# Stacked low-rank products and alternating half-array products in a recurrent branch that runs beside large matrix products

## The chip, the cores and the metric

The kernel runs on one core of one Trainium2 chip. The metric is device time in microseconds (us) of one execution, as a median over runs. The engines are named as in the profile: PE is TensorE (matrix products and transposes), DVE is VectorE, ACT is ScalarE, POOL is GpSimd, SP is SyncE, whose queue issues nearly all DMAs.

## The reference

One layer of a hybrid network on 2048 tokens of 1024 features, in fp32. The recurrent branch is cut to what the change touches.

```python
h = h_res * (1 + sc1) + sh1
proj = h @ w_in + b_in
y_a = gmlp_branch(proj[..., :1024])            # gelu, layer norm, spatial product, u * s
y_b = rwkv7_branch(proj[..., 1024:2720])
merged = sigmoid(gate_a) * (y_a @ w_branch_a) + sigmoid(gate_b) * (y_b @ w_branch_b)
h_res = layer_norm(ALPHA * h_res + gt1 * (merged @ w_out + b_out))
ff = square(relu((h_res * (1 + sc2) + sh2) @ w_ff1 + b_ff1)) @ w_ff2 + b_ff2
out = layer_norm(ALPHA * h_res + gt2 * ff)

def rwkv7_branch(z):                            # 8 heads of 64
    z = z + (shift(z) - z) * mu_shift
    r, k, v, xw, xa, xg = split(z)              # 512, 512, 512, 32, 32, 96
    decay = exp(-exp(-softplus(-(w0 + tanh(xw) @ w_decay_up)) - 0.5))
    a = sigmoid(a0 + xa @ w_aaa_up)             # low rank 32
    g = sigmoid(xg) @ w_gate_up                 # low rank 96
    kk = heads(k * k_k); kk = kk / norm(kk); k = k * (1 + (a - 1) * k_a)
    for t in tokens:                            # state per head: 64 x 64
        state = state * decay_t + (state @ -kk_t) (kk_t * a_t)^T + v_t k_t^T
        y_t = state @ r_t
    return (group_norm(y) + (r * k * r_k).sum() * v) * g
```

## The kernel before

The tokens are worked through in 4 blocks of 512 (TB), each in 4 halves of 128 (HB), each in 2 chunks of 64 (C). The 8 heads are 4 pairs (NP): an even head on partitions 0 to 63, an odd one on 64 to 127.

**Large products.** Every matrix product with a large weight is three products of fp32r operands, each operand split into a high and a low part (`mm3`, lines 453 to 455): high x high, high x low, low x high, each with 512 columns. A generator stands for each stage (`proj_rwkv`, `uv`, `gates`, `merge`, `out_proj`, `second_input`, `ff`) and yields after every 6 large products; one such step is one unit. `fetch` loads a weight tile by a DMA on SP into one of 3 buffers, ACT casts its high part (`whi`, line 387), DVE subtracts for the low part (`wlo`, line 388), again in 3 buffers each.

**Background.** The recurrent branch (`rwkv_a`, `rwkv_b`, `rwkv_c` per half) and `merge_load`, which brings the branches' results in for `merge`, are generators too. `weave` runs them between units of the large products: a background step that yields w is followed by w units (times a factor of 1.0 to 1.3 by block) before the next one. `par` lets rwkv_b of a half run beside rwkv_c of the half before and rwkv_a of the next.

- `rwkv_a` makes, for each head pair, the decays and the scaled keys. `first(p)` starts with two low-rank products of fp32 (lines 587, 588: 64 rows of the array, one PSUM tile `ua`), then works on ACT and DVE. `second(p)` makes the scores: four products (line 625) of 64 rows that use the upper (rows 0 to 63) and the lower half of the array for the even and the odd head, a product with `hones` (626), two transposes (628); DVE takes the results out of PSUM under masks (632, 633). After the pairs one product with `ind` sums the squares of the keys (648).
- `rwkv_b` inverts 32x32 triangles on DVE, then joins them by 16 products of 32x32 for the even and 16 for the odd heads, twice (712, 719: zps, tps).
- `rwkv_c` runs the chunk step: 8 products of the whole array (759, into `xy`), then 8 with the inverse (768, into `us`), 8 with BK (774) and 8 with AB (780), each set first for the even heads, then for the odd ones. A product of fp32 is two passes in the trace. Then `yp` (800, 801) per pair, and the half's result goes to DRAM (`ybd`, line 807).

PSUM has a tag "mm" of four banks for the large products and a tag "rw" of four for the small ones.

Only PE's program order is that of the code (`ORDERED`). The order of the other engines and of the DMA queues is a scheduler's. A weight tile N can be loaded and cast when PE is done with tile N - 6 (three raw and three split buffers).

Of the kernel before, what the change touches and what calls it, by code (L numbers as in the profile page):

```python
# [16 lines left out]
P = 128  # L17
# [72 lines left out]
class Body:  # L90
# [122 lines left out]
    def setup(self):  # L213
# [69 lines left out]
        self.lora = const.tile([C, 2, RW], F32, name="lora")  # L283
        nc.sync.dma_start(out=self.lora, in_=A["lora"])
# [226 lines left out]
    def proj_rwkv(self, b):  # L511
        nc, A = self.nc, self.A
        if self.h_of != b:
            self.go(self.load_h(b))
        xwa = self.work.tile([C, TB], F32, name="xwa", tag="t2", bufs=3)
        pp = self.pre[0] if b == 0 else (yield from self.fm(self.hT, m=C))
        self.shift_mix(pp, C, "xwa", 0, 12, xwa)
        nc.scalar.activation(xwa[0:32], xwa[0:32], AF.Tanh)
        xg = self.work.tile([96, TB], F32, name="xg", tag="t2", bufs=3)
        pp = self.pre[1] if b == 0 else (yield from self.fm(self.hT, m=96))  # L520
        self.shift_mix(pp, 96, "xg", 0, 13, xg)
        nc.scalar.activation(xg, xg, AF.Tanh, scale=0.5)
        nc.vector.tensor_scalar(xg, xg, 0.5, 0.5, op0=ALU.mult, op1=ALU.add)
        xd = self.dr.tile([TB // HB, C + 96, HB], F32, name="xd", tag="xd", bufs=2)
        nc.sync.dma_start(out=xd[:, 0:C].rearrange("h p t -> p h t"), in_=xwa.rearrange("p (h t) -> p h t", t=HB))
        nc.sync.dma_start(out=xd[:, C:].rearrange("h p t -> p h t"), in_=xg.rearrange("p (h t) -> p h t", t=HB))
        zd = [self.dr.tile([TB // HB, P, 3, HB], F32, name=f"zd{p}", tag=f"zd{p}", bufs=2) for p in range(NP)]
        self.spill["z", b] = (xd, zd)
# [25 lines left out]
    def rwkv_a(self, b, h, q):  # L554
# [17 lines left out]
        nc.sync.dma_start(out=xg, in_=xd[h, C:])  # L572
# [7 lines left out]

        def first(p):
            fs = slice(p * P, p * P + P)
            if b == h == 0:
                nc.sync.dma_start(out=zq[:, p], in_=zd[p][h])
            zr, zk, zv = (zq[:, p, j] for j in range(3))
            ua = pst([P, 2, HB], "ua")
            nc.tensor.matmul(ua[:, 0], lhsT=self.lora[:, 0, fs], rhs=xwa, start=True, stop=True)
            nc.tensor.matmul(ua[:, 1], lhsT=self.lora[:, 1, fs], rhs=xwa, start=True, stop=True)
            sg = w1("sg")
            nc.scalar.activation(sg, ua[:, 0], AF.Tanh, scale=0.5, bias=self.w0_h[:, p:p + 1])  # L590
            at = w1("at")
            nc.scalar.activation(at, ua[:, 1], AF.Tanh, scale=0.5, bias=self.a0_h[:, p:p + 1])
            nc.vector.tensor_scalar(sg, sg, 1.0, None, op0=ALU.add)
# [22 lines left out]
            nc.scalar.activation(ksq[:, p], zk, AF.Square, scale=self.vec("k_k", p))  # L616
# [3 lines left out]
        def second(p, bk, kp):  # L620
            zr, zk, zv = (zq[:, p, j] for j in range(3))
            s0, s1 = pst([P, 3, P], "s0"), pst([P, 4, P], "s1")
            for i, sc in enumerate((s0, s1)):
                for c in range(NC):
                    nc.tensor.matmul(sc[:, c], lhsT=bk[half[i], c], rhs=G[i][half[i], p, c], start=True, stop=True)  # L625
            nc.tensor.matmul(s0[:, NC], lhsT=self.hones, rhs=kp, start=True, stop=True)
            for c in range(NC):
                nc.tensor.transpose(s1[:, NC + c], bk[:, c], self.ident)
# [19 lines left out]
        nc.tensor.matmul(ssp, lhsT=self.ind, rhs=ksq, start=True, stop=True)  # L648
        ssq = work.tile([2, NP, HB], F32, name="ssq", tag="ssq", bufs=1)
        nc.scalar.copy(out=ssq, in_=ssp)  # L650
# [13 lines left out]
    def rwkv_b(self, q):  # L664
# [52 lines left out]
        for i, (lo, hi) in enumerate(qd):  # L717
            for u in range(U16):
# [6 lines left out]
    def rwkv_c(self, b, h, q):  # L725
# [20 lines left out]
        for c in range(NC):  # L746
# [8 lines left out]
            xy = pst([P, 2, NP, C], "xy")  # L755
# [5 lines left out]
            Xs = rp.tile([P, NP, C], F32, name="Xs", tag="Xs", bufs=1)  # L761
            nc.vector.tensor_copy(out=Xs[E], in_=xy[E, 0])
            nc.scalar.copy(out=Xs[O], in_=xy[O, 1])
            yield Y_C
            for i in range(2):
                r = half[i]
                for p in range(NP):
# [4 lines left out]
            for i in range(2):  # L772
                for p in range(NP):
# [4 lines left out]
            for i in range(2):  # L778
                for p in range(NP):
                    nc.tensor.matmul(xy[half[1 - i], i, p], lhsT=AB[half[i], p, c, cr[i]:cr[i] + C], rhs=Q[half[i], i, p],  # L780
                                     start=False, stop=True, skip_group_check=True)
            nc.vector.tensor_mul(self.Sc[self.scur], St, PC[:, c][:, :, None].to_broadcast([P, NP, C]))
            nc.scalar.copy(out=Yt[half[c], :, 0], in_=xy[O, 0])
            nc.vector.tensor_copy(out=Yt[half[c], :, 1], in_=xy[E, 1])
# [12 lines left out]
        yb = rp.tile([P, NP, HB], F32, name="yb", tag="yb")  # L797
        for p in range(NP):
            yp = pst([P, 2, HB], "yp")
            nc.tensor.transpose(yp[:, 0], Yt[:, p], self.ident)  # L800
            nc.tensor.matmul(yp[:, 1], lhsT=self.gup[:, p * P:p * P + P], rhs=xg, start=True, stop=True)
# [286 lines left out]
def arrange(np, inp):  # L1088
# [37 lines left out]
    lora = np.zeros((64, 2, 512), w.dtype)  # L1126
    lora[:32, 0] = inp["w_decay_up"][0]
    lora[32:, 1] = inp["w_aaa_up"][0]
    a["lora"] = lora
# [44 lines left out]
```

## Time and profile before

| | |
|---|---|
| time, median of 3 runs | 3103.5 us (3100.29 to 3109.51) |
| time of the profiled execution | 3111.15 us |
| its span, first to last instruction | 3109.3 us |
| mean granted clock of TensorE | 0.993 |
| PE busy (matmul) | 3046.7 us, 98% |
| PEld busy (weight load) | 2455.4 us, 79% |
| DVE busy | 2124.0 us, 68% |
| ACT busy | 1263.4 us, 41% |
| POOL busy | 149.2 us, 5% |

Matmuls overlap in the array, so a row's duration is longer than the distance to the next row's start; the distances tell the pace. An "x16" groups sixteen neighbouring instructions of one line into one row, from the first one's start to the last one's modelled end. The tile of the array that a matmul uses stands as rows*columns behind the names.

### The profile page before, as it was taken

To read this page: it belongs to the slowest core of one execution; us is meant where nothing else is said; L and a number is where in the kernel's file an instruction comes from. 1 tells how busy PE (TensorE), PEld (TensorE's weight loads), DVE (VectorE), ACT (ScalarE), POOL (GpSimd) and SP (SyncE) were. 2 spreads that over 40 slices of the span, in tenths; PEclk is the share of its full clock that TensorE was granted. 3 is DMA by queue.
4 is the path that set the end of the run, shared out by engine and by line. 5 is a ranking of instruction groups with operands and counts; after the bars stand their busy time and mean duration, and the time that the engine had idled before them with its cause. 6 is when DMAs were issued, how large, how long until landed. Compare 5 with 4: busy or idle time off the path is not lost.

```text
span 3109.3 us, 44483 instructions
## 1 busy us (share of the span) xinstructions
PE 3046.7 (98%) x16432; PEld 2455.4 (79%) x16432; DVE 2124.0 (68%) x4727; ACT 1263.4 (41%) x2012; POOL 149.2 (5%) x370
## 2 busy tenths in 40 slices
PE   8999999999999999999999999999999999999998
PEld 6776878777777877878787888787878888888887
DVE  7877874778777686486777657567668755854446
ACT  5534433353343334444433343453444334253332
POOL 1101100000000000100000000110000000000000
PEclk9999999999999999999999999999999999999999
DMA  8565544832323265433323246534333224622332
GB/s 286 158 177 165 169 135 161 271 102 86 98 82 102 82 204 190 152 129 120 104 92 93 89 142 205 164 121 148 118 97 93 84 95 146 223 88 95 98 99 95
DMA packets 241483, 416.71 MB, mean 134 GB/s; under 512 B 72465, under 2 KB 127377, under 8 KB 241265
## 3 DMA queue, kind: packets, MB, share of 16 engines
q1 hardware_dynamic: 241184, 413.59, 41.7%
q8 instruction: 130, 2.13, 0.3%
q14 instruction: 89, 0.72, 0.1%
q0 software_dynamic: 80, 0.26, 0.0%
HBM read 357.60 MB, written 56.17 MB: 133 GB/s over the span
## 4 chain that ended last, share of the span: by engine, by line
PE 85%; DVE 9%; DMA 4%; issue 1%; ACT 1%; SPq 0%; POOL 0%; DVEq 0%; ACTq 0%
PE fm_ps L453 15%; PE fm_ps L455 14%; PE fm_ps L454 14%; PE ff L453 7%; PE ff L454 7%; PE ff L455 7%; PE xy L759 2%; DVE wlo L388 1%; PE ops L454 1%; PE ops L455 1%; PE ops L453 1%; DVE tmp L687 1%; PE s L625 1%; PE vps L453 1%; PE us L768 1%
## 5 line engine op out<-in xcount | busy, mean ns | idle before, releaser
L387 ACT CAST whi<-wraw 128x1024 fp32r<-128x1024 f32 (+1 forms) x500 | 495.0, 991 | 880.7 <-PE fm_ps L454 439.5
L388 DVE TENSOR_TENSOR wlo<-wraw,whi 128x1024 fp32r<-128x1024 f32 (+1 forms) x500 | 573.0, 1148 | 343.2 <-ACT whi L387 335.7
L453 PE MATMUL fm_ps<-xh,whi 128*128 128x512 f32 x1984 | 796.1, 401 | 3.6 <-ACT xh L387 2.2
L454 PE MATMUL fm_ps<-xl,whi 128*128 128x512 f32 x1984 | 774.4, 390 | 2.8 <-DVE xl L388 2.8
L455 PE MATMUL fm_ps<-xh,wlo 128*128 128x512 f32 x1984 | 775.7, 391 | 0.6 <-DVE wlo L388 0.6
L453 PEld LDWEIGHTS fm_ps<-xh,whi 128*128 128x128 f32 x1984 | 370.8, 187 | 91.9 <-issue 5.2
L455 PEld LDWEIGHTS fm_ps<-xh,wlo 128*128 128x128 f32 x1984 | 370.8, 187 | 84.0 <-DVE wlo L388 1.5
L454 PEld LDWEIGHTS fm_ps<-xl,whi 128*128 128x128 f32 x1984 | 371.4, 187 | 77.4 <-DVE xl L388 4.3
L453 PE MATMUL ff<-hh,whi 128*128 128x512 f32 (+1 forms) x1056 | 416.2, 394 | 1.9 <-DVE zr L1051 1.2
L454 PE MATMUL ff<-hl,whi 128*128 128x512 f32 (+1 forms) x1056 | 404.8, 383 | 0.3 <-DVE hl L388 0.3
L455 PE MATMUL ff<-hh,wlo 128*128 128x512 f32 (+1 forms) x1056 | 405.1, 384 | 0.0
L1051 DVE SCALAR_TENSOR_TENSOR zr<-ff,mod,zr 128x512 f32<-128x512 f32 (+1 forms) x264 | 184.9, 730 | 138.6 <-PE ff L455 138.1
L453 PEld LDWEIGHTS ff<-hh,whi 128*128 128x128 f32 x1056 | 198.6, 188 | 46.2 <-issue 6.0
L455 PEld LDWEIGHTS ff<-hh,wlo 128*128 128x128 f32 x1056 | 198.4, 188 | 40.3
L454 PEld LDWEIGHTS ff<-hl,whi 128*128 128x128 f32 x1056 | 198.8, 188 | 35.6 <-DVE hl L388 0.5
L687 DVE TENSOR_TENSOR tmp<-T,L 128x4 f32<-128x4 f32 (+23 forms) x496 | 162.3, 327 | 10.2
L688 DVE TENSOR_REDUCE T<-tmp 128x1 f32<-128x4 f32 (+23 forms) x496 | 122.9, 248 | 10.5
L388 DVE TENSOR_TENSOR hl<-r,hh 128x512 fp32r<-128x512 f32 x128 | 87.7, 688 | 47.8 <-ACT hh L387 47.3
L454 PE MATMUL ops<-wlo,mh 128*128 128x512 f32 x256 | 103.0, 402 | 5.4 <-DVE wlo L388 5.4
L453 PE MATMUL ops<-whi,mh 128*128 128x512 f32 x256 | 102.8, 402 | 1.7 <-DVE ga L914 1.7
L453 PE MATMUL fm_ps<-yh,whi 128*128 128x512 f32 x256 | 102.2, 399 | 1.7 <-ACT yh L387 1.2
L455 PE MATMUL fm_ps<-yh,wlo 128*128 128x512 f32 x256 | 101.5, 397 | 2.0 <-DVE wlo L388 2.0
(236 smaller groups left out, 4018.9 us busy)
## 6 DMA issues: line engine op xcount, KB each, us to landing
wraw<-in_w_ff_dram SPq DMA_DIRECT2D x260, 512.0 KB
wraw<-in_w_gate_dram SPq DMA_DIRECT2D x64, 512.0 KB
wada<-in_w_ada_dram SPq DMA_DIRECT2D x48, 512.0 KB
wraw<-in_w_rkv_dram SPq DMA_DIRECT2D x42, 512.0 KB
gd<-g SPq DMA_DIRECT2D x64, 256.0 KB
ga<-gd SPq DMA_DIRECT2D x64, 256.0 KB
wraw<-in_w_out_dram SPq DMA_DIRECT2D x32, 512.0 KB
zd<-zmix SPq DMA_DIRECT2D x48, 256.0 KB
```

The costliest lines, as they stand in the source:

```text
L387: nc.scalar.copy(out=hi, in_=src)
L388: nc.vector.tensor_sub(lo, src, hi.bitcast(F32))
L453: nc.tensor.matmul(ps, lhsT=wh, rhs=xh, start=start, stop=False)
L454: nc.tensor.matmul(ps, lhsT=wh, rhs=xl, start=False, stop=False)
L455: nc.tensor.matmul(ps, lhsT=wl, rhs=xh, start=False, stop=stop)
L625: nc.tensor.matmul(sc[:, c], lhsT=bk[half[i], c], rhs=G[i][half[i], p, c], start=True, stop=True)
L687: nc.vector.tensor_mul(tmp[:, :n, :w], T[:, :n, :w], L[:, :w, t][:, None, :].to_broadcast([P, n, w]))
L688: nc.vector.tensor_reduce(T[:, :n, t:t + 1], tmp[:, :n, :w], axis=AX.X, op=ALU.add)
L759: nc.tensor.matmul(xy[:, i, p], lhsT=G[i][:, p, c], rhs=Q[:, i, p], start=(i == 0 and p == 0), stop=False, skip_group_check=True)
L768: nc.tensor.matmul(us[r, 0, p], lhsT=TT[r, p * NC + c], rhs=Xs[r, p], start=True, stop=True)
L1051: self.nc.vector.scalar_tensor_tensor(res[:, n, ts], pfs[i], self.mod[:, 40 + n:41 + n], res[:, n, ts], op0=ALU.mult, op1=ALU.add)
```

## The change

- **Low-rank products.** `proj_rwkv` splits xwa into a high and a low part (fp32r) and writes both to DRAM. The weights `lora` are stacked in four groups of 32 rows, twice the high and twice the low part, and `rwkv_a` loads xwa in four pieces to match, so that one product over 128 rows holds the high and low cross terms. For all four pairs the 8 products stand in one run at the half's start, in two PSUM tiles; ACT and DVE turn them into `sgs` and `ats`.
- **Scores.** `second` serves two pairs: 16 passes that alternate between the pair's even and odd head, then the `hones` products, the transposes, and the sums of squares (`ind`), which move here from their own run. `third` takes the results out of PSUM, pair by pair. A run holds four PSUM tiles of tag "rw". The yields change.
- **Inversion.** The two loops of zps and of tps are swapped: even and odd heads alternate.
- **Chunk step.** The 8 products of the whole array become 8 that make only the half that Xs needs (into `us[:, 1]`) and 8 that make the other half (into `xy`), alternating column halves. The loops of the other three sets are swapped so that heads alternate. One copy of 128 partitions makes Xs.
- **Output products.** The four transposes and the four gate products stand in one run with two PSUM tiles.

```diff
-        self.lora = const.tile([C, 2, RW], F32, name="lora")
-        nc.sync.dma_start(out=self.lora, in_=A["lora"])
+        self.lora = const.tile([P, 2, RW], F32R, name="lora")
+        lr = self.sp.tile([P, 2, RW], F32, name="lraw", tag="lraw")
+        for i in range(4):
+            nc.sync.dma_start(out=lr[i * 32:i * 32 + 32], in_=A["lora"])
+        nc.scalar.copy(out=self.lora, in_=lr)
+        nc.vector.tensor_sub(lr[C:], lr[C:], self.lora[C:].bitcast(F32))
+        nc.scalar.copy(out=self.lora[C:], in_=lr[C:])
...
+        parts = [self.work.tile([C, TB], F32R, name=f"xwa{n}", tag="t2", bufs=3) for n in range(2)]
+        self.split(xwa, *parts)
+        for n in range(2):
+            nc.sync.dma_start(out=xs[:, n].rearrange("h p t -> p h t"), in_=parts[n].bitcast(F32).rearrange("p (h t) -> p h t", t=HB))
...
-        xwa = rp.tile([C, HB], F32, name="xwa", tag="xwa", bufs=2)
-        nc.sync.dma_start(out=xwa, in_=xd[h, 0:C])
+        xwa = rp.tile([P, 2, HB], F32R, name="xwa", tag="xwa", bufs=1)
+        for i in range(4):
+            nc.sync.dma_start(out=xwa[i * 32:i * 32 + 32].bitcast(F32),
+                              in_=xs[h, i % 2].rearrange("(a p) t -> p a t", a=2))
...
+        uas = [pst([P, 2, 2, HB], "ua") for _ in range(NP // 2)]
+        for p in range(NP):
+            for i in range(2):
+                nc.tensor.matmul(uas[p // 2][:, p % 2, i], lhsT=self.lora[:, i, p * P:p * P + P], rhs=xwa[:, i],
+                                 start=True, stop=True)
...
-            nc.tensor.matmul(ua[:, 0], lhsT=self.lora[:, 0, fs], rhs=xwa, start=True, stop=True)
-            nc.tensor.matmul(ua[:, 1], lhsT=self.lora[:, 1, fs], rhs=xwa, start=True, stop=True)
...
+        def second(ps_, made):
+
+            sc = {p: (pst([P, 4, P], "s0"), pst([P, 4, P], "s1")) for p in ps_}
+            for p in ps_:
+                for c in range(NC):
+                    for i in range(2):
+                        nc.tensor.matmul(sc[p][i][:, c], lhsT=made[p][0][half[i], c], rhs=G[i][half[i], p, c],
+                                         start=True, stop=True)
+            for p in ps_:
+                bk, kp = made[p]
+                s0, s1 = sc[p]
+                nc.tensor.matmul(s0[:, NC], lhsT=self.hones, rhs=kp, start=True, stop=True)
+                for c in range(NC):
+                    nc.tensor.transpose(s1[:, NC + c], bk[:, c], self.ident)
+
+            for p in ps_:
+                nc.tensor.matmul(sc[p][0][0:2, NC + 1], lhsT=self.ind, rhs=ksqs[p][:, p % 2], start=True, stop=True)
+            return sc
...
-        pend = None
-        for p in range(NP + 1):
-            nxt = first(p) if p < NP else None
-            yield Y_A1
-            if pend:
-                second(p - 1, *pend)
-            pend = nxt
-            yield Y_Z2 if b == h == 0 and 0 < p < NP - 1 else Y_A2
-
-        ssp = pst([2, NP, HB], "ssp")
-        nc.tensor.matmul(ssp, lhsT=self.ind, rhs=ksq, start=True, stop=True)
...
+        for p0 in range(0, NP, 2):
+            for p in (p0, p0 + 1):
+                made[p] = first(p)
+                yield Y_A1 + (Y_Z2 if b == h == 0 and p else Y_A2)
+            sc = second((p0, p0 + 1), made)
+            for p in (p0, p0 + 1):
+                third(p, *sc[p])
+            yield Y_A2
...
-        for i, (lo, hi) in enumerate(qd):
-            for u in range(U16):
+        for u in range(U16):
+            for i, (lo, hi) in enumerate(qd):
...
-                    nc.tensor.matmul(xy[:, i, p], lhsT=G[i][:, p, c], rhs=Q[:, i, p], start=(i == 0 and p == 0),
+
+            for p in range(NP):
+                for i in range(2):
+                    nc.tensor.matmul(us[half[i], 1, p], lhsT=G[i][:, p, c, half[i]], rhs=Q[:, i, p], start=True, stop=True)
+            Xs = rp.tile([P, NP, C], F32, name="Xs", tag="Xs", bufs=1)
+            nc.vector.tensor_copy(out=Xs, in_=us[:, 1])
+            for p in range(NP):
+                for i in range(2):
+                    nc.tensor.matmul(xy[half[1 - i], p], lhsT=G[i][:, p, c, half[1 - i]], rhs=Q[:, i, p], start=p == 0,
                                      stop=False, skip_group_check=True)
...
-            for i in range(2):
-                r = half[i]
-                for p in range(NP):
+            for p in range(NP):
+                for i in range(2):
+                    r = half[i]
                     nc.tensor.matmul(us[r, 0, p], lhsT=TT[r, p * NC + c], rhs=Xs[r, p], start=True, stop=True)
```

Lines of the changed kernel: 459 to 461 are the large products, 596 the low-rank ones, 648 to 658 the score run, 744 and 751 zps and tps, 792 and 797 the split product, 803, 809 and 815 the other three sets of the chunk step.

**PE, a score run of block 0, beside the second block's projection.** Before (`fm_ps` is a large product's PSUM tile, `s` a score tile, `G` the scaled keys of even and odd heads, `bk` and `kp` the other operands):

```order
L455 MATMUL fm_ps<-xh_155,wlo 128x512
L625 MATMUL s_2850<-G_2553,bk 128x128 x2
L625 MATMUL s_2851<-G_2554,bk 128x128 x2
L626 MATMUL s_2850<-kp,hones 128x128
L628 MATMUL s_2851<-ident,bk 128x128 x2
L453 MATMUL fm_ps<-xh_2746,whi 64x512
```

Of the change, from the last two of a run's score products on (eight of two pairs):

```order
L648 MATMUL s_3198<-G_2640,bk 128x128
L648 MATMUL s_3199<-G_2641,bk 128x128
L653 MATMUL s_3196<-kp,hones 128x128
L655 MATMUL s_3197<-ident,bk 128x128 x2
L653 MATMUL s_3198<-kp,hones 128x128
L655 MATMUL s_3199<-ident,bk 128x128 x2
L658 MATMUL s_3196<-ksq,ind 2x128
L658 MATMUL s_3198<-ksq,ind 2x128
L459 MATMUL fm_ps<-xh_2757,whi 128x512
```

One head pair between two large products has become two, with the sums of squares at the end, before the next large product.

**ACT, where the first block's inputs have arrived.** `first` are the PSUM tiles of the opening products, `zraw`, `xwa`, `xg`, `zmix` the mixed inputs made from them, `whi` the high part of a weight tile. Before:

```order
L387 CAST xh_155<-ht 128x512
L387 CAST whi<-wraw 128x1024 x2
L506 ACTIVATE zraw<-first_164,vecs 64x512
L508 ACTIVATE xwa<-first_164,mix 64x512
L506 ACTIVATE zraw<-first_165,vecs 96x512
L508 ACTIVATE xg<-first_165,mix 96x512
L518 ACTIVATE xwa<-xwa 32x512
L506 ACTIVATE zraw<-first_166,vecs 128x512
L522 ACTIVATE xg<-xg 96x512
L508 ACTIVATE zmix<-first_166,mix 128x512
L506 ACTIVATE zraw<-first_167,vecs 128x512
L387 CAST whi<-wraw 128x1024
```

Of the change:

```order
L512 ACTIVATE zraw<-first_164,vecs 64x512
L514 ACTIVATE xwa<-first_164,mix 64x512
L288 CAST lora<-lraw 128x1024
L524 ACTIVATE xwa<-xwa 32x512
L512 ACTIVATE zraw<-first_165,vecs 96x512
L514 ACTIVATE xg<-first_165,mix 96x512
L290 CAST lora<-lraw 64x1024
L528 ACTIVATE xg<-xg 96x512
L393 CAST xwa_558<-xwa 64x512
L512 ACTIVATE zraw<-first_166,vecs 128x512
L512 ACTIVATE zraw<-first_167,vecs 128x512
L393 CAST whi<-wraw 128x1024 x3
```

The casts of the first two weight tiles stood ahead of the first `zraw`; they stand behind it and ten more operations now, among them two casts of `lora` and one of `xwa`.

**SP, the end of block 0.** `wraw<-in_w_a_dram` and `wraw<-in_w_b_dram` are merge's weight fetches in turn, the first of them the 69th tile of the program; `yld` and `uld` are merge_load's loads, `ga` merge's gates, `wada` the modulation weights. Before, from the fourth load of `sd` to merge's fourth weight tile:

```order
L895 DMA yld<-sd 128x512
L375 DMA wada<-in_w_ada_dram 128x1024
L896 DMA uld<-ud 128x512
L899 DMA yld<-ybd 128x512
L912 DMA ga<-gd 128x512
L446 DMA wraw<-in_w_a_dram 128x512
L899 DMA yld<-ybd 128x512
L375 DMA wada<-in_w_ada_dram 128x1024
L880 DMA gd<-g 128x512
L899 DMA yld<-ybd 128x512 x2
L446 DMA wraw<-in_w_b_dram 128x512
```

Of the change, from just ahead of merge's sixth weight tile to its seventh:

```order
L949 DMA ga<-gd 128x512
L950 DMA ga<-gd 128x512
L934 DMA uld<-ud 128x512
L452 DMA wraw<-in_w_b_dram 128x512
L933 DMA yld<-sd 128x512
L934 DMA uld<-ud 128x512
L918 DMA gd<-g 128x512
L937 DMA yld<-ybd 128x512 x3
L381 DMA wada<-in_w_ada_dram 128x1024
L937 DMA yld<-ybd 128x512
L452 DMA wraw<-in_w_a_dram 128x512
```

The last four loads of `ybd` stood before merge's fourth weight fetch; they stand behind its sixth.

## Rows read from the trace of the kernel before

**Rows 1.** The page, part 1: busy time, share of the span, instructions.

```profile
PE 3046.7 (98%) x16432; PEld 2455.4 (79%) x16432; DVE 2124.0 (68%) x4727; ACT 1263.4 (41%) x2012; POOL 149.2 (5%) x370
```

**Rows 2.** Timeline of PE around a run of line 768: start, duration (us), instructions.

```profile
1004.01 0.39 PE L454 MATMUL ff<-hl,whi 128*128 128x512 f32 x1
1004.24 0.39 PE L455 MATMUL ff<-hh,wlo 128*128 128x512 f32 x1
1004.55 0.96 PE L768 MATMUL us<-Xs,TT 64*64 64x64 f32 x16
1005.45 0.50 PE L453 MATMUL ff<-hh,whi 128*128 128x512 f32 x1
1005.78 0.39 PE L454 MATMUL ff<-hl,whi 128*128 128x512 f32 x1
```

**Rows 3.** Timeline of PE in three narrow windows inside that run: passes in flight.

```profile
1004.84 0.44 PE L768 MATMUL us<-Xs,TT 64*64 64x64 f32 x7
...
1005.12 0.39 PE L768 MATMUL us<-Xs,TT 64*64 64x64 f32 x4
...
1005.24 0.28 PE L768 MATMUL us<-Xs,TT 64*64 64x64 f32 x2
```

**Rows 4.** Timeline of PE around lines 774 and 780.

```profile
1008.41 0.97 PE L774 MATMUL us<-Q,BK 128*64 128x64 f32 x16
1009.30 0.96 PE L780 MATMUL xy<-Q,AB 64*64 64x64 f32 x16
```

**Rows 5.** Timeline of PE around line 759.

```profile
999.92 1.89 PE L759 MATMUL xy<-Q,G 128*128 128x64 f32 x16
1001.62 0.48 PE L453 MATMUL ff<-hh,whi 128*128 128x512 f32 x1
```

**Rows 6.** Timeline of PE around an inversion run.

```profile
1543.33 1.09 PE L712 MATMUL zps<-T,AB 32*32 32x32 f32 x32
```

**Rows 7.** Timeline of PE around a low-rank run.

```profile
1508.61 0.48 PE L587 MATMUL ua<-xwa,lora 64*128 64x128 f32 x2
...
1509.25 0.50 PE L453 MATMUL ff<-hh,whi 128*128 128x512 f32 x1
```

**Rows 8.** Timeline of PE around the transposes of v.

```profile
1567.25 0.60 PE L738 MATMUL vt<-ident,zq 128*128 128x128 f32 x4
1567.60 0.48 PE L453 MATMUL ff<-hh,whi 128*128 128x512 f32 x1
```

**Rows 9.** Timeline of PE around a score run.

```profile
1522.59 0.72 PE L625 MATMUL s<-G,bk 64*128 64x128 f32 x8
1523.24 0.49 PE L626 MATMUL s<-kp,hones 128*128 128x128 f32 x2
...
1523.70 0.48 PE L453 MATMUL fm_ps<-xh,whi 128*128 128x512 f32 x1
```

**Rows 10.** Timeline of PE around the sums of squares.

```profile
1564.80 1.02 PE L648 MATMUL ssp<-ksq,ind 128*2 128x512 f32 x2
```

**Rows 11.** Timeline of ACT and of PE where the first block's inputs end.

```profile
56.48 0.69 ACT L506 ACTIVATE zraw<-first,vecs 64x512 f32<-64x512 f32 x1 [4.13 <-PE first L455]
...
61.14 0.39 PE L453 MATMUL fm_ps<-xh,whi 128*128 128x512 f32 x1
```

**Rows 12.** Timeline of PE at the second block's first product; brackets: idle time, releaser.

```profile
283.46 0.69 PE L454 MATMUL fm_ps<-xl,whi 128*64 128x512 f32 x1 [2.21 <-DVE xl L388]
```

**Rows 13.** Windows: length, busy of PE, PEld, DVE, ACT, POOL, then granted clock, DMA.

```profile
282.50:289.20 6.70, 5.74 (x15) 3.15 (x15) 5.99 (x12) 3.79 (x7) 0.00 (x0) 0.50 0.47 152
```

**Rows 14.** Timeline of SP, DVE and PE at the end of block 0.

```profile
543.71 0.32 SPq L896 DMA_DIRECT2D uld<-ud  x1
...
548.36 0.69 DVE L388 TENSOR_TENSOR yl<-yld,yh 128x512 fp32r<-128x512 f32 x1 [0.69 <-ACT yh L387]
...
558.74 0.40 PE L453 MATMUL fm_ps<-yh,whi 128*128 128x512 f32 x1
```

**Rows 15.** Groups of instructions of DVE: busy us, mean ns, idle before, releasers.

```profile
L632 DVE TENSOR_TENSOR AB<-s,mask_e 64x256 f32<-64x256 f32 x64 | 26.4, 413 | 17.4 <-PE s L626 16.7
```

More of the change, by code (lines that the diff above doesn't have):

```diff
@@ L615, in first, with third @@
                 nc.vector.tensor_mul(bk[r, :, cr[i]:cr[i] + C], ch(kp)[r], ch(pinv)[r])
-            nc.scalar.activation(ksq[:, p], zk, AF.Square, scale=self.vec("k_k", p))
+            nc.scalar.activation(ksq[:, p % 2], zk, AF.Square, scale=self.vec("k_k", p))
             nc.vector.scalar_tensor_tensor(kp, kp, self.vec("r_k", p), zr, op0=ALU.mult, op1=ALU.mult)
             return bk, kp
-        def second(p, bk, kp):
-            zr, zk, zv = (zq[:, p, j] for j in range(3))
[L622 to L628, printed above, removed]
+        def second(ps_, made):
[14 more added lines that the diff above has]
+            return sc
+        def third(p, s0, s1):
+            zr, zk, zv = (zq[:, p, j] for j in range(3))
             for i, sc in enumerate((s0, s1)):
@@ L636, in second @@
             nc.scalar.copy(out=BK[:, p], in_=s1[:, NC:])
-        pend = None
-        for p in range(NP + 1):
-            nxt = first(p) if p < NP else None
-            yield Y_A1
-            if pend:
-                second(p - 1, *pend)
-            pend = nxt
-            yield Y_Z2 if b == h == 0 and 0 < p < NP - 1 else Y_A2
-        ssp = pst([2, NP, HB], "ssp")
-        nc.tensor.matmul(ssp, lhsT=self.ind, rhs=ksq, start=True, stop=True)
-        ssq = work.tile([2, NP, HB], F32, name="ssq", tag="ssq", bufs=1)
-        nc.scalar.copy(out=ssq, in_=ssp)
+            nc.scalar.copy(out=ssq[:, p], in_=s0[0:2, NC + 1])
+        ssq = work.tile([2, NP, HB], F32, name="ssq", tag="gsq", bufs=1)
+        made = {}
+        for p0 in range(0, NP, 2):
[6 more added lines that the diff above has]
+            yield Y_A2
         U = NP * NC
@@ L716, in rwkv_b @@
         yield Y_V2
-        for i, (lo, hi) in enumerate(qd):
-            for u in range(U16):
+        for u in range(U16):
+            for i, (lo, hi) in enumerate(qd):
                 nc.tensor.matmul(tps[lo, u], lhsT=Zs[hi, u], rhs=TT[hi, u, 32:64], start=True, stop=True)
@@ L777, in rwkv_c @@
             self.scur ^= 1
-            for i in range(2):
-                for p in range(NP):
-                    nc.tensor.matmul(xy[half[1 - i], i, p], lhsT=AB[half[i], p, c, cr[i]:cr[i] + C], rhs=Q[half[i], i, p],
+            for p in range(NP):
+                for i in range(2):
+                    nc.tensor.matmul(xy[half[1 - i], p], lhsT=AB[half[i], p, c, cr[i]:cr[i] + C], rhs=Q[half[i], i, p],
                                      start=False, stop=True, skip_group_check=True)
             nc.vector.tensor_mul(self.Sc[self.scur], St, PC[:, c][:, :, None].to_broadcast([P, NP, C]))
-            nc.scalar.copy(out=Yt[half[c], :, 0], in_=xy[O, 0])
-            nc.vector.tensor_copy(out=Yt[half[c], :, 1], in_=xy[E, 1])
+            nc.scalar.copy(out=Yt[half[c], :, 0], in_=xy[O])
+            nc.vector.tensor_copy(out=Yt[half[c], :, 1], in_=xy[E])
         yv = Yt.rearrange("p k h i -> p (k h) i")
@@ L797, in rwkv_c @@
         yb = rp.tile([P, NP, HB], F32, name="yb", tag="yb")
+        yps = [pst([P, 2, 2, HB], "yp") for _ in range(NP // 2)]
         for p in range(NP):
-            yp = pst([P, 2, HB], "yp")
-            nc.tensor.transpose(yp[:, 0], Yt[:, p], self.ident)
-            nc.tensor.matmul(yp[:, 1], lhsT=self.gup[:, p * P:p * P + P], rhs=xg, start=True, stop=True)
+            nc.tensor.transpose(yps[p // 2][:, p % 2, 0], Yt[:, p], self.ident)
+        for p in range(NP):
+            nc.tensor.matmul(yps[p // 2][:, p % 2, 1], lhsT=self.gup[:, p * P:p * P + P], rhs=xg, start=True, stop=True)
+        for p in range(NP):
+            yp = yps[p // 2][:, p % 2]
             y1 = rp.tile([P, HB], F32, name="y1", tag="t1", bufs=1)
```

51 lines of the change are left out of this document (24 added, 27 removed).

## The prediction

> **What bounds the kernel now.** The page's busy times come first: PE, TensorE's matmul queue, is busy for 98% of the span [rows 1]. There is almost no idle time to win, so a gain has to come from fewer or cheaper PE instructions, and any new wait of PE costs its full length. The next view is PE's timeline, row by row around one small run. The large products (N=512) follow each other every 0.23 us. A run of small ones between two of them starts 0.31 us after the last large one instead of 0.23, when it uses only part of the array, and the first large product behind it needs 0.33 until its follower starts [rows 2]. I price every run as entry + its own time to the first large product + exit - 2 x 0.23, that is, as what PE would save if the run vanished.
>
> The same view shows how parts of the array work together. In the run of line 768 eight products use the upper left quarter of the array, then eight the lower right one. Asked for narrow windows, the timeline gives 4 passes in flight near the end, where only the second quarter works, and two of them start within 0.12 us, so 0.06 apart; near the middle, where the end of one set meets the start of the other, it gives 7 [rows 3]. Passes have the same length, so both quarters were working at once, at nearly double rate. The queue reaches ahead only a little, so most of each set still runs alone. Alternating the quarters should give the double rate throughout.
>
> **The change, part by part.**
>
> Chunk step (32 of them: 4 blocks, 4 halves, 2 chunks).
> - Line 768 now costs 0.31 + 0.90 + 0.33 - 0.46 = 1.08 us [rows 2]. Alternated: 8 pairs of passes at 0.06 = 0.48, plus 0.09 behind the last (1005.12 to 1005.45 less four passes [rows 2, 3]) and about 0.05 for the first, so 0.31 + 0.62 + 0.33 - 0.46 = 0.80. Saves 0.28 x 32 = 9.0.
> - Lines 774 and 780 stand in one run: 0.89 and, less a tail of 0.06 as in rows 2, 0.90 us [rows 4], 1.98 with entry and exit. Alternated, 0.62 each: 1.42. Saves 0.56 x 32 = 17.9.
> - Line 759 (full array, 64 columns of output per pass) takes 1.70 [rows 5], with entry 0.23 and exit 0.33 1.80. It becomes 32 passes of half the array's columns, in 16 pairs: 0.96 + 0.14, with entry and exit 1.28. Saves 0.52 x 32 = 16.6.
>
> Inversion (zps and tps, 32 runs). 32 passes take 1.09 us less 0.06 of tail [rows 6], 1.21 with entry and exit. At 0.032 per pass, 16 pairs take 0.51 + 0.14, with entry and exit 0.83. Saves 0.38 x 32 = 12.2.
>
> Low-rank products. A run of lines 587 and 588 takes 0.64 us [rows 7], 0.82 with entry and exit, and there are 64: 52.5. Now 8 one-pass products with the whole array make one run per half. No row shows an fp32r pass of 128 columns. The nearest is the transpose, one pass of the same tile: four take 0.35 [rows 8], so eight 0.70, 0.80 with entry and exit, x 16 = 12.8. Saves 39.7. Bounds: at a quarter of a 512-column pass each (0.06) they would save 44; as dear as the old products (0.64 / 2) they would save 10. I take the transpose, since it has the same tile and the same single pass.
>
> Scores. A run for one head pair takes 1.11 us to the next large product [rows 9], 1.29 with entry and exit, 64 times; the sums of squares (ssp) take 0.95 after their tail [rows 10], 1.14 in all, 16 times: together 100.8. The new run serves two pairs: 2 x 1.11, less one change of tile shape (an estimated 0.20: eight passes take 0.65 to line 626, of which 0.45 go at the average pace of rows 4), plus that change and about 0.32 for the four narrow passes of ind, and 0.10 more behind a narrow tile: 2.82 with entry and exit, x 32 = 90.2. Saves 10.6. The score passes already alternate quarters, so alternation gives nothing here.
>
> The output products (yp) keep their passes in fewer runs; with a full-array entry at the normal spacing I count nothing. The 32 Xs copies that ACT loses and the DVE copy that gets 128 partitions are hidden behind the twelve large products between two runs; without that cover they cost about 0.3 each, 10 us. Each half's four loads of xwa instead of one, and each block's extra write and split, go to SP, ACT and DVE before PE asks for them, but for the first half (below).
>
> Work removed: 9.0 + 17.9 + 16.6 + 12.2 + 39.7 + 10.6 = 106 us.
>
> New waits, against it.
> - Start. In ACT's new order eleven operations stand ahead of the first weight cast, which used to run before them. The first starts at 56.48 after waiting for PE, and PE needs the weights at 61.14 [rows 11]. Nine at about 0.65 (0.69 with the overlap) and two double-width casts at an estimated 1.0 end at 64.4, the cast at 65.4, plus the VectorE half: about 5 us late. Behind a pause of 2.21 us at the second block's first product [rows 12] the granted clock stood at 0.50, the lower of its two levels (1.2 and 2.4 GHz), for 6.7 us [rows 13]; that costs 3.35 in full, 1.7 for half the stretch. The low-rank run also waits for its new loads, queued on SP behind weight fetches. I take 8 us in all, between 3 and 12.
> - End of blocks 0 and 1. rwkv_a has 28 units instead of 25, so the last yp of block 0 comes 60 large products later, 48 before merge. SP's order shows what follows: the last loads of y stand behind merge's sixth weight fetch, whose buffers come free when PE is done with the last gates tile, which is when merge starts (558.74). From a load of u to the end of its split took 543.71 to 549.05, 5.3 us [rows 14]; with the queue ahead of it 7, and 2.5 for the clock (between 0 and 3.35). Block 1 has the same shape. Together 19, between 5 and 25. Blocks 2 and 3 have over 200 large products of slack.
> - Middle. A pair run takes all four banks of the tag "rw", and rwkv_b, rwkv_c and the next run ask for the same four. They come free after third: four products at 0.41 [rows 15] and about 0.3 for the last, 2.0 us of DVE per head pair, 4.0 per run. The next asker is mostly 2 to 5 units (1.4 us each) behind, but DVE is also doing splits and inversions. I take 0.3 per run, 10 us, between 0 and 64.
>
> The sum is 8 + 19 + 10 = 37 of waits, -69 net. The profiled execution took 3111.15 (span 3109.3), so 3042 for it; it lies 7.6 above the median of the runs, 3103.5, so I predict 3035.
>
> A rule of the Trainium skill speaks against the alternation. TensorEngine Tiling (Array Packing), Restrictions and Gotchas, Gotcha 1, says that different row tiles cannot access the same PSUM bank simultaneously. Lines 768, 780 and the inversions write one bank from two row tiles. The seven passes in flight speak against it here: there the row tiles wrote one bank, in different partitions. By the row these three save 9.0, 9.0 and 12.2; by the rule it is the rival "row tiles take turns" below.
>
> **The rivals.**
> - Waits stay hidden (0.12). For it: nearly every wait of PE now is short, and background work has slack. Against it: the ACT order at the start. -106: 2998.
> - Banks wait (0.07): each pair run exposes one pair's evacuation, 2.0 x 32 = 64 in place of 10: -106 + 27 + 64 = -15, 3088. For it: all four banks are held. Against it: the askers stand some units behind.
> - Banks wait in full, the other side (0.04): all 4.0 us of third stand in PE's way at each of 32 runs, 128: +49, 3152. It decides from 2.5 us per run on ((106 - 27) / 32).
> - Row tiles take turns (0.02): lines 768 and 780 then cost 16 x 0.06 + 0.14 in place of 0.90, 0.20 more each, the inversions 0.13 more, each x 32, and they save nothing: -106 + 30 + 17 + 37 = -22, 3082. Rows 3 speak against it.
> - No overlap at all (0.02): the runs of 759 and 774 lose theirs as well, so the split of 759 costs 0.44 x 32 = 14 and 774 0.21 x 32 = 7 instead of saving 16.6 and 9: -106 + 30 + 17 + 26 + 21 + 37 = +25, 3128. Rows 3 speak against it, and so does 774: its two sets of eight take 0.89, less than 16 x 0.06 + 0.14.
>
> **How the numbers follow.** The forecast, gain of 106 against waits of 20 to 60 and dearer low-rank passes, has 0.70 and its own range 3013 to 3062. 0.03 is for what I have not seen. The range over all reaches to 2997 (half of the hidden-waits case) and to 3080; left out are the other half, most of the bank cases, and the last rival, about 0.2. A measurement of this kernel can tell about 0.3%, 9 us, from no change. Faster than 3094: the forecast, hidden waits, row tiles and most of one pair's banks, 0.90; within 9 us 0.04; slower 0.06.
>
> **What would show it.** The run of 803 at 0.6 us from its first pass to the next large product, that of 809 with 815 at about 1.3, that of 792 with 797 near 1.1, the eight low-rank products near 0.7: each is right or wrong by itself in PE's timeline. The waits: PE idle for the first weights near 61 us, idle at the first product of merge in blocks 0 and 1, with granted clock 0.50 behind each. If PE's waits name s, zps or xy banks through DVE for tens of us, the bank case holds. The forecast is wrong if 792 and 797 take more than 1.7 us, or if waits sum to over 100.

## The result and the profile after

The changed kernel takes 3072.1 us (median of 4 runs, 3068.8 to 3075.0) against 3104.4 before; the ratio is 0.9895, 95% interval 0.9877 to 0.9913. That is a gain of 32 us, less than half of the 69 forecast. The profiled execution took 3075.0 with a span of 3073.3, 36.0 under the span of before.

The page's busy times, which answer to [rows 1]:

```profile
PE 2963.9 (96%) x16912; PEld 2396.8 (78%) x16912; DVE 2127.0 (69%) x4684; ACT 1247.6 (41%) x2028; POOL 157.0 (5%) x370
```

PE is busy 83 us less, but the span is only 36 shorter: 47 us of idle time are new. The timeline of PE shows the runs themselves, in the second half of the span, where nothing waits (start, duration, instructions):

```profile
1482.41 0.68 PE L803 MATMUL us<-Xs,TT 64*64 64x64 f32 x16
1483.02 0.50 PE L459 MATMUL fm_ps<-xh,whi 128*128 128x512 f32 x1
...
1485.97 0.69 PE L809 MATMUL us<-Q,BK 128*64 128x64 f32 x16
1486.58 0.68 PE L815 MATMUL xy<-Q,AB 64*64 64x64 f32 x16
1487.19 0.50 PE L459 MATMUL fm_ps<-xh,whi 128*128 128x512 f32 x1
...
1510.47 1.00 PE L596 MATMUL ua<-xwa,lora 128*128 128x128 f32 x8
1511.31 0.44 PE L459 MATMUL ff<-hh,whi 128*128 128x512 f32 x1
...
1533.24 1.16 PE L648 MATMUL s<-G,bk 64*128 64x128 f32 x16
1534.33 0.49 PE L653 MATMUL s<-kp,hones 128*128 128x128 f32 x2
1534.66 0.38 PE L655 MATMUL s<-ident,bk 128*128 128x128 f32 x2
1534.87 0.39 PE L653 MATMUL s<-kp,hones 128*128 128x128 f32 x2
1535.10 0.38 PE L655 MATMUL s<-ident,bk 128*128 128x128 f32 x2
1535.41 0.60 PE L658 MATMUL s<-ksq,ind 128*2 128x128 f32 x4
1535.94 0.50 PE L459 MATMUL fm_ps<-xh,whi 128*128 128x512 f32 x1
...
1542.97 0.69 PE L744 MATMUL zps<-T,AB 32*32 32x32 f32 x32
1543.59 0.50 PE L459 MATMUL ff<-hh,whi 128*128 128x512 f32 x1
...
1573.92 0.69 PE L792 MATMUL us<-Q,G 128*64 128x64 f32 x16
1574.43 0.64 PE L797 MATMUL xy<-Q,G 128*64 128x64 f32 x16
1575.00 0.50 PE L459 MATMUL fm_ps<-xh,whi 128*128 128x512 f32 x1
```

From a run's first pass to the next large product: 803 takes 0.61 (forecast 0.62; [rows 2] 0.90), 809 with 815 1.22 (1.24; [rows 4] 1.79), 792 with 797 1.08 (1.10; [rows 5] 1.70), the inversion 0.62 (0.65; [rows 6] 1.03), the eight low-rank products 0.84 (0.70). The score run of two pairs takes 2.70, 2.90 in all where 2.82 was forecast. With these figures the work removed is 9 + 18 + 17 + 12 + 38 + 8 = 102 us, not 106. That side came out nearly as priced; of the 102, 66 us were lost elsewhere, since the span is 36 shorter.

Where, the windows tell. The stretches end where PE starts the first large product of merge in block 0, of second_input in block 0, of merge in block 1, of block 2's projection, of merge in blocks 2 and 3. Before:

```profile
0.00:558.74 558.74, 533.79 (x3064) 420.41 (x3065) 409.54 (x1074) 236.34 (x392) 55.08 (x142) 0.99 0.58 180
558.74:658.03 99.29, 92.34 (x396) 72.85 (x394) 73.71 (x125) 33.56 (x47) 2.42 (x7) 1.00 0.64 212
658.03:1115.87 457.84, 453.76 (x2702) 364.37 (x2703) 352.67 (x906) 192.95 (x350) 15.84 (x41) 0.99 0.32 98
1115.87:1218.60 102.73, 96.95 (x417) 77.21 (x416) 83.96 (x141) 39.14 (x56) 4.10 (x8) 0.97 0.63 210
1218.60:1880.30 661.70, 660.66 (x3643) 532.11 (x3642) 434.25 (x991) 277.10 (x445) 30.66 (x78) 1.00 0.37 116
1880.30:2639.10 758.80, 755.17 (x4058) 608.64 (x4057) 514.17 (x1126) 313.47 (x495) 34.24 (x83) 1.00 0.40 128
```

After (columns as in [rows 13]: length, busy of PE, PEld, DVE, ACT, POOL, then granted clock):

```profile
0.00:557.04 557.04, 515.20 (x3184) 407.52 (x3184) 406.70 (x1061) 233.59 (x396) 52.58 (x142) 0.97 0.57 179
557.04:668.90 111.86, 98.62 (x395) 74.90 (x395) 77.78 (x129) 35.59 (x49) 2.42 (x7) 0.91 0.61 203
668.90:1114.10 445.20, 430.44 (x2823) 348.09 (x2823) 352.84 (x893) 189.37 (x354) 22.05 (x41) 0.98 0.33 97
1114.10:1225.20 111.10, 99.77 (x416) 78.42 (x417) 85.28 (x143) 39.78 (x57) 3.87 (x7) 0.92 0.65 211
1225.20:1865.20 640.00, 635.47 (x3761) 515.71 (x3760) 434.21 (x980) 271.10 (x448) 32.91 (x78) 1.00 0.39 120
1865.20:2603.00 737.80, 730.16 (x4178) 592.15 (x4177) 514.64 (x1115) 307.33 (x498) 36.29 (x83) 1.00 0.43 132
```

Each of stretches 1, 3, 5 and 6 holds one block's recurrent branch and lost 102 / 4 = 25.5 us of work. They are shorter by 1.7, 12.6, 21.7 and 21.0; the two around merge, which lost no work, are longer by 12.6 and 8.4. So the shortfall is 24 in block 0, 13 in merge behind it, 13 in block 1, 8 in its merge, and 4 and 5 in the last two. Of the first 24 and the 13 of block 1, 3.5 and 1.1 are a wait for y just ahead of merge's first product, which the windows count to the stretch before it. Behind merge of block 3 the two kernels run alike. In the short stretches the granted clock is lower too: 0.91 and 0.92 at the two merges, against 1.00 and 0.97.

Three places where PE waits, from its timeline: the first weights, the first low-rank run, and the start of merge in block 0, five times there (idle time and releaser in brackets):

```profile
64.10 0.79 PE L459 MATMUL fm_ps<-xh,whi 128*128 128x512 f32 x1 [3.66 <-ACT whi L393]
...
75.70 0.78 PE L596 MATMUL ua<-xwa,lora 128*128 128x128 f32 x4 [1.84 <-DMA xwa<-xs]
...
557.04 0.58 PE L459 MATMUL fm_ps<-yh,whi 128*128 128x512 f32 x1 [3.49 <-ACT yh L393]
...
563.36 0.79 PE L459 MATMUL fm_ps<-yh,whi 128*128 128x512 f32 x1 [4.36 <-ACT yh L393]
...
567.23 0.80 PE L459 MATMUL fm_ps<-yh,whi 128*128 128x512 f32 x1 [1.92 <-ACT yh L393]
...
571.04 0.79 PE L459 MATMUL fm_ps<-yh,whi 128*128 128x512 f32 x1 [1.86 <-ACT yh L393]
...
574.08 0.79 PE L459 MATMUL fm_ps<-yh,whi 128*128 128x512 f32 x1 [1.09 <-ACT yh L393]
```

The granted clock (column behind POOL) at the first and the third of them, from the windows:

```profile
62.38:69.20 6.82, 4.89 (x11) 3.40 (x12) 5.12 (x6) 5.09 (x8) 1.47 (x4) 0.50 0.60 152
557.31:577.79 20.48, 11.00 (x20) 5.40 (x20) 9.05 (x15) 5.01 (x8) 0.00 (x0) 0.50 0.68 237
```

At merge four tiles of y come one after the other, the second 6 us behind the first, the next two 4 us apart, while PE needs all four for its first twelve products. Through these 20.5 us the clock is at 0.50.

In block 1 PE waits 6.05 us for a PSUM bank of the feed-forward sum, which `zr` on DVE has to take out. DVE's timeline shows what stood ahead of `zr`: the evacuation of a pair run (taking its results out of PSUM, 666 to 669) between steps of the inversion (719, 720), without a pause. The last of it, of DVE, then of PE:

```profile
785.24 0.43 DVE L666 TENSOR_TENSOR AB<-s,mask_o 64x256 f32<-64x256 f32 x1
785.70 0.60 DVE L719 TENSOR_TENSOR tmp<-T,L 128x256 f32<-128x256 f32 x1
786.32 0.42 DVE L667 TENSOR_TENSOR G<-s,mask_o 64x256 f32<-64x256 f32 x1
786.66 0.40 DVE L720 TENSOR_REDUCE T<-tmp 128x8 f32<-128x256 f32 x1
786.99 0.27 DVE L669 TENSOR_TENSOR zq<-s,zq 128x128 f32<-128x128 f32 x1
787.19 1.39 DVE L1089 SCALAR_TENSOR_TENSOR zr<-ff,mod,zr 128x512 f32<-128x512 f32 x2
...
788.07 0.77 PE L459 MATMUL fm_ps<-xh,whi 128*128 128x512 f32 x1 [6.05 <-DVE zr L1089]
```

### The profile page after: what moved, and what is told of

Same layout as the page of the kernel before. It is cut to its first block, busy times and chain, and to the rows that moved or that the text cites. A ratio compares the mean times of both kernels' runs of the same rounds, so it can differ in the third digit from the quotient of the medians.

```text
span 3073.3 us, 45399 instructions
## 1 busy us (share of the span) xinstructions
PE 2963.9 (96%) x16912; PEld 2396.8 (78%) x16912; DVE 2127.0 (69%) x4684; ACT 1247.6 (41%) x2028; POOL 157.0 (5%) x370
## 4 chain that ended last, share of the span: by engine, by line
PE 57%; DVE 3%; DMA 1%; ACT 1%; issue 0%; SPq 0%; DVEq 0%; ACTq 0%
PE fm_ps L459 10%; PE fm_ps L460 10%; PE fm_ps L461 10%; PE ff L459 6%; PE ff L460 6%; PE ff L461 6%; PE ops L460 1%; PE ops L461 1%; PE ops L459 1%; DVE wlo L394 1%; PE s L648 1%; PE vps L459 0%; PE vps L461 0%; PE vps L460 0%; PE pf L460 0%
## 5 line engine op out<-in xcount | busy, mean ns | idle before, releaser
L460 PE MATMUL fm_ps<-yl,whi 128*128 128x512 f32 x256 | 105.2, 411 | 1.4 <-DVE yl L394 1.1
```

The source lines that it names most:

```text
L460: nc.tensor.matmul(ps, lhsT=wh, rhs=xl, start=False, stop=False)
```

## The experiments

Times are medians of runs beside the kernel before on the same chip (3102.3 to 3106.6 by group); a gain is against that.

**The chunk step and the inversion alone.** The kernel before with the changed loops of `rwkv_b` and of the chunk step, as in the diff above, and nothing else.

> The kernel before with the chunk step and the inversion of the change, nothing else. Theory W (the work comes off as priced, and the waits that ate it belong to the pair runs of scores with their later output products): the runs save (1.99 + 1.79 + 1.09 - 1.43 - 1.28 - 0.81) x 32 = 43 and 0.40 x 32 = 13, and nearly no wait is added: 3104 - 56 = 3048, at most 3057. Rival F (a faster PE by itself runs into DVE, ACT and the loads, whatever part makes it faster): half of it is lost, 3062 to 3080.

3056.7, a gain of 47.6 (ratio 0.9841, 0.9824 to 0.9858): most of the 56, as W has it and not F, and 15 us faster than the whole change. By stretch block 0 takes 543.2 and merge behind it 97.0, and block 1 takes 446.7: blocks 0 and 1 gave back 15.5 and 11.2 of the 14 that each lost in work, though DVE is busy for 75% and 79% of them.

**The low-rank products alone.**

```diff
+        uas = [pst([P, 2, 2, HB], "ua") for _ in range(NP // 2)]
...
-        ksq = rp.tile([P, NP, HB], F32, name="ksq", tag="ksq", bufs=1)
+        ksq = ats
```

> The kernel before with the stacked low-rank products alone (splits, loads and setup of the change; scores of one pair per run; squares of the keys go into the tile of the second tanh once it is used). W: saves (0.84 x 64 - 0.90 x 16) = 39, loses about 10 at the start (late weight cast, late load, clock): 3075. Rival F: 3085 to 3095. Rival L (the extra loads and splits of this part carry the waits of the change): 3095 or more, with PE waiting for xwa in many halves.

3093.6, a gain of 10.7 of 39. W missed by 19, and PE waits for xwa only once, 1.7 us, so L does not hold as it was put; the result lies in F's range.

**The change without the pair runs.** `second(p, bk, kp)`, the loop with `pend` and `ssp` as before.

> The change with the scores as before (one pair per run, sums of squares apart, yields of 25 units per half; squares as in the run above). W: 56 + 39 of work saved, 10 to 15 of waits at the start and in between, no train of waits at the first products of merge in blocks 0 and 1: 3020 to 3026. Rivals F and L: the waits stay, 3050 to 3075.

3064.3, a gain of 40.1. The trains at merge (waits for y, one behind the other) are gone (101.7 and 99.6 us for the two merge stretches), as W has it, but two parts that gain 47.6 and 10.7 alone gain 40.1 together. The pair runs, priced at 8 us of gain, cost 8: by stretch 10.1 and 11.5 at the two merges and 1.0 and 4.1 in blocks 0 and 1, while blocks 2 and 3 take 8.0 and 6.4 longer without them. The time lies in F's range and not in W's. But of the 20 us that the two parts together lack in the profiles, 12 are in blocks 2 and 3, where each has one new wait for `zr`, with a granted clock of 0.74 over the next 6.6 us and of 0.62 over the next 6.7:

```profile
1604.46 0.47 PE L459 MATMUL fm_ps<-xh,whi 128*128 128x512 f32 x1 [4.39 <-DVE zr L1075]
...
2347.82 0.77 PE L459 MATMUL fm_ps<-xh,whi 128*128 128x512 f32 x1 [5.39 <-DVE zr L1075]
```

Such a wait needs neither a pair run nor the blocks in which DVE is fullest.

**A tighter background.**

```diff
-LAT0 = 1.05
-LAT1 = 1.0
+LAT0 = 1.0
+LAT1 = 0.95
```

> The change with the background of blocks 0 and 1 set 5% tighter (LAT0 1.05 to 1.0, LAT1 1.0 to 0.95), so that the last output products come 78 and 72 large products earlier, 18 and 36 earlier than in the kernel before. W: the trains of waits at merge in blocks 0 and 1 (13.5 and 9.9 us idle, with the clock halved behind) go, some of it comes back as waits of scores for DVE: 3045 to 3055. Rival: the trains have another cause (loads late for SP's queue, not for the output products), 3068 to 3075.

3047.3, a gain of 57.0, 25 us better than the change. The merge stretches take 98.5 and 100.8, so the trains are gone, and merge of block 0 starts without a wait:

```profile
556.05 0.39 PE L461 MATMUL fm_ps<-xh,wlo 128*128 128x512 f32 x1
556.28 0.40 PE L459 MATMUL fm_ps<-yh,whi 128*128 128x512 f32 x1
```

The trains came of the output products' place: the last of block 0 stand 126 large products ahead of merge here, 48 in the change, 108 in the kernel before.

**The setup of lora early.** The load, casts and subtraction of `lora` stand ahead of `self.first_tiles()`; tried on the change, on the low-rank part alone, on the change with the tighter background, and on the change without pair runs.

```diff
+        nc.scalar.copy(out=self.lora, in_=lr)
+        nc.vector.tensor_sub(lr[C:], lr[C:], self.lora[C:].bitcast(F32))
+        nc.scalar.copy(out=self.lora[C:], in_=lr[C:])
         self.first_tiles()
```

> The change with the load, casts and subtraction of lora written ahead of the opening products, so that ACT's casts of the first two weight tiles stand ahead of the first zraw again. Theory S (the late weight casts at 61 us start a backlog of ACT, loads and clock that runs on through block 0): most of the 25 us that block 0 fell short up to merge come back, 3052 to 3060. Rival D (block 0 falls short since DVE, ACT and SP have as much to do per large product there as PE, whatever the start): only the start's own wait and clock come back, some 6 us, 3064 to 3068.

> The kernel before with the stacked low-rank products alone, their setup ahead of the opening products. Priced: 39 us of work. S: 3070 to 3080, with block 0 no longer behind the kernel before at its merge. D: 3084 to 3090.

> The change with the tighter background of blocks 0 and 1 (LAT0 1.0, LAT1 0.95) and the setup of lora early. If the trains of waits at merge and the start are apart, both gains add: 3047 less 12 to 20 by S, 3028 to 3036; less 6 by D, 3039 to 3043.

> The change with scores of one pair per run as before and the setup of lora early. S: 3064 less 12 to 20, 3044 to 3052, which would be the best without touching the background's pace. D: 3056 to 3060.

3070.2, 3087.8, 3042.1 and 3057.1: 2, 6, 5 and 7 us better than without. The wait of 3.66 for the first weights is gone, but the opening products start 2.1 to 2.6 us later, and the first low-rank run waits longer for xwa (3.83 in place of 1.66 in the low-rank part alone). Theory S, a backlog that runs on from the late weight casts, falls: with them in time little comes back. The edit moved part of the start's loss to xwa and did not remove it.

**DVE relieved.** Every second step of the inversion is left out, in the change and, as a control, in the kernel before; the 32x32 inverses are then not computed in full.

```diff
-        for t in range(1, 32):
+        for t in range(1, 32, 2):
```

> The change with every second step of the triangle inversion left out (two DVE operations each; about 34 us of DVE per block; the inverse is not computed in full, the yields and PE's order stay). Theory D (in blocks 0 and 1 PE waits since DVE's queue is nearly as full as PE's): the waits for bk, for zr and for Yt shrink, block 0 and block 1 each get 5 to 12 us faster: 3072 to 3050 or lower. Rival P (the waits come from loads, ACT and PE's order alone): 3068 to 3074.

> The control: the kernel before with the same steps left out. D: PE there waits little for DVE (some 10 us in the background's stretches), so it gains at most 8 us, clearly less than the change does: 3096 to 3103. If it gains as much as the change, DVE's load is not what the change runs into.

The change comes to 3045.2, 27 us less; the control to 3094.4, 12 less. The difference is in blocks 0 and 1: their stretches shrink by 15.6 and 13.3 us in the change, by 8.1 and 5.4 in the control. In the change PE's waits (total, times, longest) name DVE's `bk` and `zr`:

```profile
PE s L648 <- DVE bk L637: 6.4, 6, 2.4
PE fm_ps L459 <- DVE zr L1089: 6.1, 1, 6.1
```

With DVE relieved that for `bk` is not in the list any more, and that for `zr` is halved:

```profile
PE fm_ps L459 <- DVE zr L1089: 3.2, 1, 3.2
```

The merge stretches stay as long (111.7 and 110.1), so they are another matter. D holds, for about 15 of the 37 us that blocks 0 and 1 fell short (28.9 less the control's 13.5). The control gained more than D had it (12, not 8): DVE held PE up a little before as well.

**Tiles of their own for the loads of y.**

```diff
-            y = work.tile([P, TB], F32, name="yld", tag="t2", bufs=3)
+            y = bp.tile([P, TB], F32, name="yld", tag=f"ml{k}")
...
-                u = work.tile([P, TB], F32, name="uld", tag="t2", bufs=3)
+                u = bp.tile([P, TB], F32, name="uld", tag=f"mh{k}")
```

> The change with tiles of their own for the loads of y and u before merge (in the space of the merge results, which are not yet made) in place of the three that everything shares. Theory T (the waits at merge's start are four loads in a row, each waiting for the tiles of the one before): the trains of 13.5 and 9.9 us become one wait each, 6 to 8 us, with less half clock behind: 3072 less 15 to 25, 3047 to 3057. Rival Q (SP's queue holds the loads back, behind weight fetches): 3066 to 3074.

3058.1, 14 us better than the change; T at block 0, less than it gave in all. At merge of block 0 the train is a wait of 3.35 and small ones, at that of block 1 one of 8.21:

```profile
556.35 0.51 PE L459 MATMUL fm_ps<-yh,whi 128*128 128x512 f32 x1 [3.35 <-ACT yh L393]
...
557.68 0.80 PE L460 MATMUL fm_ps<-yl,whi 128*128 128x512 f32 x1 [0.82 <-DVE yl L394]
...
560.81 0.80 PE L459 MATMUL fm_ps<-yh,whi 128*128 128x512 f32 x1 [0.63 <-ACT yh L393]
...
1112.23 0.79 PE L459 MATMUL fm_ps<-yh,whi 128*128 128x512 f32 x1 [8.21 <-ACT yh L393]
```

The merge stretches take 103.7 and 107.1. The wait of 8.21 counts to the stretch ahead of merge, which grows from 445.2 to 452.2, so block 1 with its merge is 3 us longer than in the change, and block 0 with its merge 9 shorter. The stretches of blocks 2 and 3 shrink too, 640.0 to 635.8 and 737.8 to 730.5, which is their full price: there `ff` had shared its three tiles with the late loads of y, and its two waits of 1.7 for `hh` are gone.

**Together, and kp on ACT.** Early setup, tighter background, own tiles, and

```diff
-            nc.vector.tensor_scalar(kp, at, self.ka_h[:, p:p + 1], self.ka_c[:, p:p + 1], op0=ALU.mult, op1=ALU.add)
+            nc.scalar.activation(kp, at, AF.Identity, scale=self.ka_h[:, p:p + 1], bias=self.ka_c[:, p:p + 1])
```

> The change with the early setup of lora, the tighter background (3042 together), the own tiles for y and u, and the scaling of kp moved from DVE to ACT (64 operations, 21 us of DVE). D and T: 5 to 10 us under 3042 by the lighter DVE, nearly nothing by the tiles since the output products already come in time there: 3032 to 3038. P: 3040 to 3044.

3025.5 (ratio 0.9736, 0.9721 to 0.9750), better than expected: a gain of 81 against 102 of work removed. How much of the 17 us over the version without the last two edits belongs to either was not tried apart; in the profiles blocks 2 and 3 give 4.3 and 6.4 of it, about what the own tiles gave there alone.

**The low-rank part once more, by pair and with DVE relieved; the fastest version started later.** The first keeps two stacked products per head pair at their old places, each pair's in a PSUM tile of its own.

> The kernel before with the stacked low-rank products, setup early, but two products per head pair at the places of before, in a PSUM tile each. By rows a run of two costs about 0.3 (0.23 + 0.2 + 0.32 - 0.46) x 64 = 19 in place of 52, so 33 priced against 39 in one run per half. Theory U (the run of eight takes two banks at once at the half's start, waits for them and for xwa, and is why the low-rank part alone returned 16 of 39): 3070 to 3078. Rival D (the stretch is short of DVE and ACT time whatever the places): 3084 to 3094.

> The low-rank part alone with early setup (3088), with every second step of the triangle inversion left out. The same edit took 10 to 12 off the kernel before and 27 off the change. D: clearly more than 12 off, 3064 to 3072. U: 10 to 12 off, 3075 to 3078.

> The fastest version so far (3026) with the first half's background started three units later (Y_Z 4 to 7), so that the first low-rank run does not wait 5.7 us for xwa. If that wait and the half clock behind it are all, 3017 to 3021; if the later start is only passed on to the waits behind, 3024 to 3028.

3088.1, as with one run per half: U falls, the place and the banks are not the cause. With DVE relieved 3073.3, 14.5 less, hardly more than the control's 12 and in neither theory's range: the low-rank part's own shortfall is not shown to be DVE's. By stretch (early setup) it is in block 0, 562.4 against 558.7 before, where 10 had to come off, and some 3 us in block 1; blocks 2 and 3 gain their 10 each. Set against the kernel before product by product, it falls behind in three steps: 6 us where the first low-rank run waits 3.83 for xwa, 5 where the spatial product waits 3.02 for `u` on ACT and the next product 1.51 for `sv` on DVE, and 5 where the next low-rank run waits 2.28 and, for `yb` on DVE, 1.68. The later start brings block 0's merge forward by 6.5 us in the profile and the time to 3023.3 from 3025.5, too little to tell: stretches 2, 3 and 6 of its profile are longer by 1.2, 2.8 and 2.5 us.

## Why the prediction was wrong

The mechanism and the price of the work stood; the size of the waits did not: 66 us in place of 37, most of the difference in one term.

- **Work removed.** Alternation gave the double rate at once, in all four places: 56 of 56 us by the runs' rows. The low-rank products took 0.84 in place of 0.70, the score runs 2.90 in place of 2.82: 102 in place of 106. That the score passes of before already alternate is misread: their order shows two products of the even head, then two of the odd. Alternated, sixteen passes take 1.09 where two runs of eight took 1.30; the prediction had taken 0.2 off there for a saved change of tile shape, and the rows do not tell the two apart. The rivals "row tiles take turns" and "no overlap at all" are out, and with the former the rule of the Trainium skill (TensorEngine Tiling (Array Packing), Restrictions and Gotchas, Gotcha 1) as a limit of time: the sixteen passes of 803 wrote one bank from two row tiles in 0.61.
- **Start.** Forecast 8 (3 to 12), found 3.66 and 1.84 of waits with a lower clock behind each. The 61st large product starts 0.9 us earlier than before, the 241st, just behind both, 9.5 later: 10.4 in all. Right in place, and in its range.
- **End of blocks 0 and 1.** Forecast 19 (5 to 25), found 12.6 + 8.4 = 21 by stretch, and 25.5 with the waits of 3.5 and 1.1 just ahead of merge's first product. The place was right, the mechanism half: not one late load with its clock, but up to five waits in a row, since y and u take turns in three shared tiles.
- **Middle.** This is the step that failed: "I take 0.3 per run, 10 us". Block 0 fell 24 short, of which 10.4 are the start and 3.5 merge's first wait; block 1 13, less 1.1 for the same; the last two blocks 8: together 30 in place of 10. The prediction spread the cost evenly over 32 pair runs and looked for it in the "rw" banks. It is not even: of the 8 in blocks 2 and 3 own tiles for y gave all back, so that was the shared tiles. Of the 22 in the middle of blocks 0 and 1 about 15 go back to DVE's load by the relief. In the longest wait there PE stood for no bank of "rw" at all, but for one of the feed-forward sum, whose evacuation came behind a pair's evacuation and steps of the inversion on DVE.

Of the rivals, "waits stay hidden" is out, and "banks wait" had the nearer time (3088) with the wrong resource. That DVE's busy share decides is not shown: it is 73% and 79% in blocks 0 and 1 against 68% and 70% in the last two, but the chunk step and the inversion alone gave back 15.5 and 11.2 of 14 at 75% and 79%, and the waits for `zr` without pair runs fell in blocks 2 and 3. What stays open: the other 7 us in the middle of blocks 0 and 1, and the cause of the low-rank part's 14 in block 0, of which neither its place nor DVE alone is the cause. Its first step is a wait for the load of xwa; why PE waits at the other two is not shown.

## What to carry to other kernels

Price the runs of the engine that bounds by start-to-start distances in its timeline; that was right to 4%. Price the waits by stretch, not per instruction: where the second engine is busy for three quarters of the time, here in blocks 0 and 1, this change gave back 14 of 51 us, and relieving that engine about 15 more. The busy share alone does not foretell it, since one part of the change by itself got nearly all of its saving back in the same stretches; ask of each bank that the first engine needs next what stands ahead of its evacuation. When background work is re-paced, look at what the last step before each barrier still has ahead of it, and how many buffers its loads share: here a change of two pacing numbers was worth 25 us.

## What the runs showed of the hardware

Passes that use different quarters or halves of the array ran at the double rate as soon as they alternated, also where they wrote one PSUM bank in different partitions (803: 16 passes in 0.61 us, against 0.90; two passes start every 0.058 us, where one did while a single set ran). An fp32r pass of 128 columns took 0.84 / 8 = 0.105 us, nearly half of the 0.23 of one of 512 columns and a little more than a transpose of that tile ([rows 8], 0.35 / 4). The waits cost twice: through the train at merge the granted clock stood at 0.50, the lower level, for 20.5 us, in which PE was busy for 11.0.
